# A hybrid backbone block: the context's split input moves to GLA's workspace, and its projections are computed together with those of segments 0 and 1

## The chip, the cores and the metric

The kernel runs on one core of one Trainium2 chip. Its time is the device time in microseconds. PE is TensorE, DVE is VectorE, ACT is ScalarE, POOL is GpSimd, SP is SyncE, whose queue issues most of the DMAs.

## The reference, cut to what matters

One layer works on 2048 latent tokens and on a context of 256 tokens, 1024 features each. Both are normalized, modulated by an adaLN vector (context and latent have their own) and multiplied by one combined input matrix. Its columns feed three mixers: gated linear attention (GLA: q, k, v, decay ranks, gate gg), a gated linear recurrence with a short convolution (RG-LRU: lx, gate lg) and a state-space layer (S5: su).

```python
for d in range(N_DIR):
    ...
    yc, h_ctx = run(d, ci, None)      # the context is scanned alone
    yl, _ = run(d, li, h_ctx)         # the latent scan starts from its final state
```

After the mixers come an output projection, a second norm and an MLP with squared ReLU. The context's own outputs are not needed, so of its columns only su, lx, v and k are computed.

## The kernel before, in words

The tokens are cut into the context "c" (256 tokens) and segments 0 to 3 of 512 tokens. Features lie on partitions, in eight tiles of 128 (KT). Every operand of a large product is split into two fp32r parts, high and low, and a product of 1024 features by 128 columns is 8 x 3 = 24 matmuls (`mm3`, L323 to L326: high x high, high x low, low x high).

**The input's preparation** (`h_of`, `hprep`): 256 tokens are loaded (L287), squared on ACT (L291), summed on DVE (L292, L294), summed over partitions on PE (L296), made into a factor on ACT (L298, L299); DVE multiplies (L302), ACT writes the high part hH (L303), DVE the low part hL (L307). A segment takes two such halves, the context one. The load tile x has one buffer, so a half is loaded only when the half before it is finished. hH and hL come from `big_pair()`, two buffers each, and the context takes one of the two.

**The weights** (`wsplit`): a tile of 128 x 1024 (512 KB) is loaded by SP (L318), its high part written by ACT (L319), its low part by DVE (L320). There are two buffers for the load and the high part, three for the low part.

**The order of the work.** `in_proj` is the main stream: it goes through a plan, a list of (names, chunks) written by hand; ("h", s) prepares a chunk, and every other entry computes for each name, and in it for each chunk, one weight tile's product into one of two PSUM tiles acc. v0 and v1 are computed token block by token block (272 columns: 256 values and 16 decay ranks). Side streams (S5's preparation `s5_prep`, GLA's `gla_prep`, RG-LRU, `mod_rest` with the rest of the adaLN weights) are woven in by the time that the main stream has yielded, and each waits for the names of the chunks that it reads. The scheduler of the language then fixes one order for each engine; priorities (HP, WP) put preparation and weight splits ahead. What comes later (read-out, output projection, MLP) follows the first phase.

**GLA's workspace.** `wg` hands out tiles of 128 x 1024 floats, four buffers (YS). `gla_prep` takes three of them for the context and four for each pair of blocks; for a pair it runs L895 on PE, then ACT, DVE and POOL, then transposes L928 on PE. `gla_prep("c")` is the first of GLA's stream and needs v0, v1, k0 and k1 of the context.

Of the kernel before, what the change touches and what calls it, by code (L numbers as in the profile page):

```python
# [8 lines left out]
F32 = mybir.dt.float32  # L9
# [7 lines left out]
P = 128  # L17
D = 1024
KT = 8
# [4 lines left out]
NS = 16          # S5 groups  # L24
T8 = 8           # tokens that share a column of the S5 input layout
T16 = 16         # S5 chunk
NCH = SEQ // T16  # latent chunks
CCH = CTX // T16  # context chunks
NP = T16 + 2     # powers of the transition
XSZ = 1312  # L30
PKW = 1408       # S5 matrices of a group: read-out 2 x 256, input 4 x 128, kernel 3 x 128
# [11 lines left out]
# columns of the packed per-feature vector table  # L43
# [9 lines left out]
# W_in column tiles of 128 features  # L53
COLS = ["su0", "su1", "lx0", "lx1", "k0", "k1", "q0", "q1", "gg0", "gg1", "gg2", "gg3", "lg0", "lg1"]
WIDX = {n: i for i, n in enumerate(COLS)}
VN = 272         # half of v and the decay ranks of one direction


class Streams:
    """Emits a main and several side streams of instructions in step.  # L60

    A stream yields the time that its step takes, or the name of an event that has to be emitted first."""
# [10 lines left out]
    def step(self, limit):  # L73
        """One step of the side stream that is furthest behind; False if none is ready before `limit`."""
        ready = [x for x in self.live if (x[3] is None or x[3] in self.done) and (limit is None or x[2] <= limit)]
        if not ready:
            return False
        x = min(ready, key=lambda y: y[2])
        x[3] = None
        try:  # L80
            r = next(x[0])
        except StopIteration:
            self.live.remove(x)
            return True
        if isinstance(r, str):
            x[3] = r
        else:
            x[2] += r * x[1]
        return True

    def run(self, main):
        """`main` with the side streams."""
# [20 lines left out]
def chain(*gens):  # L113
    for g in gens:
        yield from g
# [3 lines left out]
def hybrid_block(ctx: ExitStack, tc: tile.TileContext, xT, ctxT, cc, cct, wmodA, wmodT, pv, win, wva, wvb, upw, lrini, lruw, s5v, gluw,  # L119
# [27 lines left out]
    # ---------------------------------------------------------------- constants  # L147
# [14 lines left out]
    gsc1 = consts.tile([P, 16], F32, name="gsc1")      # norm1*(1+sc1): latent, context  # L162
    gsc2 = consts.tile([P, 8], F32, name="gsc2")

    # DRAM scratch, one tile per token segment
# [22 lines left out]
    qq_d = dram.tile([8, P, 1024], F32, name="qq_d")      # by pairs of blocks  # L188
    kk_d = dram.tile([8, P, 1024], F32, name="kk_d")
    ds_d = dram.tile([NB, 64, 512], F32, name="ds_d")      # backward block updates  # L190
    sf_d = dram.tile([16, 64, 512], F32, name="sf_d")      # forward states that enter the blocks
    bs_d = dram.tile([64, 512], F32, name="bs_d")          # backward state carried to the next segment
    # constant rows and borders of the scratch
# [7 lines left out]
    # ---------------------------------------------------------------- pools of the first phase  # L201
# [4 lines left out]
    def slots(tag, size, bufs):  # L206
        """A rotating workspace of `bufs` slots of `size` floats a partition."""
# [19 lines left out]
    def big_pair():  # L227
        """The two parts of a split operand of 512 tokens."""
# [4 lines left out]
    # ---------------------------------------------------------------- adaLN vectors  # L233
# [3 lines left out]
    # silu(c) on every partition, for the products that run along the free axis  # L237
# [8 lines left out]
    def mod_first():  # L246
        """shift and scale of the first norm, latent and context"""
# [35 lines left out]
    # ---------------------------------------------------------------- normalized, modulated, split input  # L283
    def hprep(pool, src, t0, n, hH, hL, gsc, sh):
        """Normalize and modulate n tokens of src and split them exactly into two fp32r parts."""
        x = pool.tile([P, KT, n], F32, name="x", tag="x", bufs=XB)
        S.dma_start(x, src[:, t0:t0 + n].rearrange("(k p) t -> p k t", p=P))  # L287
        # 1/rms over the features on every partition
# [20 lines left out]
    def wsplit(pool, src, shape, tag, bufs, parts=None):  # L309
        """Load a weight tile and split it exactly into two fp32r parts (in `parts`, if they are there already);  # L310
        bufs: of the load, of each part."""
# [16 lines left out]
    # ---------------------------------------------------------------- input projection  # L328
# [30 lines left out]
    def h_of(s):  # L359
        n = seg_n(s)  # L360
        hH, hL = (t[:, :, :n] for t in big_pair())
        hh[s] = (hH, hL)
# [6 lines left out]
    def v_cols(c, chunks):  # L369
        """Half of the values, token by token, with the decay ranks of one direction."""  # L370
# [50 lines left out]
    # ---------------------------------------------------------------- RG-LRU  # L421
# [21 lines left out]
    def lru(d, order, wl=wl):  # L443
        for s in order:
# [31 lines left out]
            # gates; sigmoid(z) = (1 + tanh(z/2))/2  # L476
# [35 lines left out]
    # ---------------------------------------------------------------- S5  # L512
# [4 lines left out]
    def s5_params():  # L517
# [73 lines left out]
        def cmul(or_, oi, ar, ai, br, bi, t, conj_b=False, neg_i=False):  # L591
            """(or, oi) = a*b (conj(b) if conj_b); oi negated if neg_i."""
# [51 lines left out]
        # step[k] = e^{+-i theta T 2^k}: + on the forward half, - on the backward half  # L644
# [7 lines left out]
        # input matrix  # L652
# [20 lines left out]
        # powers by slot: E: forward j, backward 17-j;  F: forward 15-s, backward s  # L673
# [13 lines left out]
    def s5_prep(b):  # L687
# [5 lines left out]
        # C lambda^k by slot  # L693
# [22 lines left out]
        # intra-chunk kernel, both directions  # L716
# [11 lines left out]
        # shifted windows of it make the Toeplitz blocks  # L728
# [9 lines left out]
    def s5_tables(g0):  # L738
        """Phase tables of four groups by doubling."""
# [23 lines left out]
    def s5_run(g):  # L763
# [32 lines left out]
        # real scans; results shifted by one chunk so that a chunk's column holds the state that enters it  # L796
# [9 lines left out]
        # the state that enters latent chunk c sits at column c + CCH + 1 on both halves  # L806
# [25 lines left out]
    # ---------------------------------------------------------------- GLA, first part: decays and block states  # L832
# [18 lines left out]
    def gla_prep(s, blocks, other=False):  # L851
        """Decays, decayed queries and keys, block updates, forward states of pairs of blocks of a segment.

        other: in the memory that the input's norm has left."""
# [15 lines left out]
        for b in blocks:  # L870
# [19 lines left out]
            # -log_sigmoid(z) = max(-z, 0) + log(1 + exp(-|z|))  # L890
# [49 lines left out]
            # forward states  # L940
# [16 lines left out]
    def gla_ends():  # L957
        """-log_sigmoid of the (shifted) token past the end of each sequence"""
# [15 lines left out]
    # ================================================================ read-out and MLP  # L974
# [15 lines left out]
    def ws(s, n, tag="t"):  # L990
        """Workspaces of the read-out, n tiles of 512; the last segment's come before the MLP's memory is there."""
# [11 lines left out]
    def decays():  # L1003
        # exponents of the decay between a block's anchor and the state that enters it
        # forward: -c_mid/16; backward: -(c_127 - c_mid + c_0 of the next block)/16
# [14 lines left out]
    def back_step(ss, blk):  # L1020
        """backward state that enters latent block blk -> ss[64:128]"""
# [17 lines left out]
    def open_ff():  # L1039
        """The first phase's workspaces make room for the MLP's."""  # L1040
# [8 lines left out]
    def read_out(s):  # L1049
        """Read-out of the three groups of a segment."""  # L1050
# [6 lines left out]
        # GLA read-out, pairs of blocks from the last to the first as the backward state runs  # L1057
# [55 lines left out]
        # RG-LRU gate  # L1113
# [14 lines left out]
        # S5 gate  # L1128
# [24 lines left out]
    def out_proj(s):  # L1153
        """Output projection, residual and second norm of a segment."""
        early = []
        if s == 3:
            # the first products run while the S5 group's read-out comes to its end
# [33 lines left out]
        # second norm; its split result takes the place of the split read-out  # L1191
# [102 lines left out]
    # ================================================================ first phase  # L1294
# [149 lines left out]
```

## Time and profile before

| | |
|---|---|
| median of 3 runs | 2480.51 us (2476.4 to 2482.62) |
| profiled execution, its span | 2482.1 us, nothing around it |
| PE busy | 2347.2 us, 95%, 10992 matmul records |
| PE weight loads busy | 1886.0 us, 76% |
| DVE busy | 1610.0 us, 65% |
| ACT busy | 1169.2 us, 47% |
| POOL busy | 100.7 us, 4% |
| PE share of the chain that ended last | 64% |

The profiled execution lies 1.6 us above the median and within the runs. Busy shares are means over a first phase (to about 850 us), in which all engines work, and the MLP after it, which is nearly all PE.

### The profile page before, as it was taken

The numbers are of one execution on the slowest core, as the hardware profiler recorded it, in microseconds if no ns is written. First come the engines' busy times: TensorE is split into PE (matmuls) and PEld (weight loads), VectorE is DVE, ScalarE is ACT, GpSimd is POOL, SyncE is SP. The second block draws the span as 40 slices with busy tenths as digits, with TensorE's granted clock in tenths as the row PEclk, the third lists the DMA queues.
The fourth block names the chain that finished last, engine by engine and source line by source line (L and its number), as shares of the span: only waits on it lengthen the run. The fifth ranks groups of instructions, "written<-read, shape, count | busy, mean of one in ns | idle before, by whom it ended". The sixth has DMA issues, their size and how long they took to land.

```text
span 2482.1 us, 29891 instructions
## 1 busy us (share of the span) xinstructions
PE 2347.2 (95%) x10992; PEld 1886.0 (76%) x10992; DVE 1610.0 (65%) x2698; ACT 1169.2 (47%) x1704; POOL 100.7 (4%) x141
## 2 busy tenths in 40 slices
PE   7779999898887899999999999999999999999997
PEld 3668777877675677888877788887778888888886
DVE  6886878726786766565576656557655655655555
ACT  3764567436555645343355534336543433433333
POOL 1020111002100000000000000000000000000000
PEclk9989999999998999999999999999999999999999
DMA  7666777557775643322355322336522232333221
GB/s 258 209 201 208 223 238 227 168 174 207 253 240 181 206 135 120 101 94 93 100 177 162 118 86 93 102 102 202 159 85 94 94 102 87 126 102 102 94 94 51
DMA packets 189107, 364.03 MB, mean 147 GB/s; under 512 B 35200, under 2 KB 104144, under 8 KB 187920
## 3 DMA queue, kind: packets, MB, share of 16 engines
q1 hardware_dynamic: 183872, 346.20, 44.1%
q0 software_dynamic: 5088, 15.93, 1.9%
q8 instruction: 86, 1.41, 0.2%
q14 instruction: 61, 0.50, 0.1%
HBM read 299.76 MB, written 62.75 MB: 146 GB/s over the span
## 4 chain that ended last, share of the span: by engine, by line
PE 64%; ACT 5%; DVE 5%; DMA 3%; issue 2%; SPq 1%; POOL 0%; DVEq 0%; ACTq 0%; POOLq 0%
PE acc L324 10%; PE acc L326 9%; PE acc L325 9%; PE sa L324 9%; PE sa L325 9%; PE sa L326 9%; PE sb L324 2%; PE sb L326 2%; PE sb L325 2%; DVE wL L320 1%; ACT wH L319 1%; PE sb L1146 1%; DMA t<-lru 1%; DMA t<-kk_d 0%; DMA wR<-in_wout_dram 0%
## 5 line engine op out<-in xcount | busy, mean ns | idle before, releaser
L319 ACT CAST wH<-wR 128x1024 fp32r<-128x1024 f32 (+1 forms) x353 | 370.9, 1051 | 903.9 <-PE sa L325 432.8
L324 PE MATMUL acc<-hH,wH 128*128 128x512 f32 (+1 forms) x1576 | 629.6, 400 | 24.8 <-ACT hH L303 9.2
L320 DVE TENSOR_TENSOR wL<-wR,wH 128x1024 fp32r<-128x1024 f32 (+1 forms) x353 | 427.3, 1222 | 346.5 <-ACT wH L319 342.0
L326 PE MATMUL acc<-hH,wL 128*128 128x512 f32 (+1 forms) x1576 | 620.1, 394 | 3.2 <-DVE wL L320 3.1
L325 PE MATMUL acc<-hL,wH 128*128 128x512 f32 (+1 forms) x1576 | 617.7, 392 | 1.2 <-DVE hL L307 0.8
L1257 DVE SCALAR_TENSOR_TENSOR xa<-sa,modl,xa 128x512 f32<-128x512 f32 (+1 forms) x520 | 383.1, 741 | 197.5 <-PE sa L326 194.8
L324 PE MATMUL sa<-sH,wH 128*128 128x512 f32 (+1 forms) x1040 | 403.9, 389 | 4.6 <-DVE xa L1257 4.2
L326 PE MATMUL sa<-sH,wL 128*128 128x512 f32 (+1 forms) x1040 | 402.2, 387 | 0.0
L325 PE MATMUL sa<-sL,wH 128*128 128x512 f32 (+1 forms) x1040 | 401.9, 386 | 0.0
L324 PEld LDWEIGHTS acc<-hH,wH 128*128 128x128 f32 x1576 | 299.8, 191 | 95.3 <-ACT hH L303 10.3
L325 PEld LDWEIGHTS acc<-hL,wH 128*128 128x128 f32 x1576 | 300.1, 191 | 70.8 <-issue 6.2
L326 PEld LDWEIGHTS acc<-hH,wL 128*128 128x128 f32 x1576 | 299.5, 190 | 70.8 <-DVE wL L320 5.2
L324 PEld LDWEIGHTS sa<-sH,wH 128*128 128x128 f32 x1040 | 195.2, 188 | 49.2 <-DVE xa L1257 9.3
L326 PEld LDWEIGHTS sa<-sH,wL 128*128 128x128 f32 x1040 | 195.3, 188 | 40.8
L325 PEld LDWEIGHTS sa<-sL,wH 128*128 128x128 f32 x1040 | 195.4, 188 | 40.6 <-DVE sL L1233 0.8
L1233 DVE TENSOR_TENSOR sL<-sr,sH 128x512 fp32r<-128x512 f32 x128 | 88.2, 690 | 27.6 <-ACT sH L1232 27.5
L325 PE MATMUL acc<-wL,hH 128*128 128x272 f32 x288 | 87.8, 305 | 8.8 <-DVE wL L320 8.7
L324 PE MATMUL acc<-wH,hH 128*128 128x272 f32 x288 | 89.2, 310 | 2.0 <-ACT ev L331 1.9
L331 ACT COPY ev<-acc 128x512 f32<-128x512 f32 (+2 forms) x96 | 47.5, 495 | 85.1 <-issue 41.0
L326 PE MATMUL acc<-wH,hL 128*128 128x272 f32 x288 | 86.5, 301 | 0.0
L1232 ACT CAST sH<-sr 128x512 fp32r<-128x512 f32 x128 | 78.8, 617 | 10.8 <-PE sa L326 9.0
L1231 ACT ACTIVATE sr<-sr 128x512 f32<-128x512 f32 x128 | 80.8, 632 | 3.4
(402 smaller groups left out, 2717.2 us busy)
## 6 DMA issues: line engine op xcount, KB each, us to landing
wR<-in_w_dram SPq DMA_DIRECT2D x256, 512.0 KB
wR<-in_win_dram SPq DMA_DIRECT2D x54, 512.0 KB
wm<-in_wmodT_dram SPq DMA_DIRECT2D x32, 512.0 KB
wR<-in_wout_dram SPq DMA_DIRECT2D x32, 512.0 KB
wm<-in_wmodA_dram SPq DMA_DIRECT2D x8, 1024.0 KB
x<-in_xT_dram SPq DMA_DIRECT2D x8, 1024.0 KB
w<-pk_d SPq DMA_DIRECT2D x16, 512.0 KB
xa<-in_xT_dram SPq DMA_DIRECT2D x32, 256.0 KB
```

Source lines behind the costliest of these rows:

```text
L319: A.copy(Hf, raw)
L320: V.tensor_tensor(Lf, raw, f32(Hf), OP.subtract)
L324: T.matmul(acc, wH, hH, start=first, stop=False)
L325: T.matmul(acc, wH, hL, start=False, stop=False)
L326: T.matmul(acc, wL, hH, start=False, stop=last)
L331: A.copy(e, acc)
L1146: T.matmul(ps, gw[:, k, ct * P:(ct + 1) * P], sg[k], start=k == 0, stop=k == 1)
L1231: A.activation(r, r, AF.Square)
L1232: A.copy(sH, r)
L1233: V.tensor_tensor(sL, r, f32(sH), OP.subtract)
L1257: V.scalar_tensor_tensor(xa[:, m, a0:a1], acc, modl[:, 40 + m:41 + m], xa[:, m, a0:a1], OP.mult, OP.add)
```

## The change: what it does

The context's hH and hL no longer come from `big_pair()`. They are put into GLA's four wg tiles, each part in two halves of four feature tiles, which the new class `Halves` indexes like one tile. Segments 0 and 1 so have both big pairs from the start. The plan is rewritten: A4 (su0 su1 lx0 lx1) runs for the context and segment 0 with one split of each weight tile, v0 v1 k0 k1 for the context, segment 0 and segment 1, then q0 q1 for segments 0 and 1, and then A4 for segment 1. From G4 of segment 0 on the plan is as before. Other lines of the diff only drop comments.

```diff
+class Halves:
+    def __init__(self, tiles):
+        self.tiles = tiles
+    def __getitem__(self, at):
+        p, k, t = at
+        if isinstance(k, slice):
+            return Halves([x[p, :, t] for x in self.tiles])
+        return self.tiles[k // 4][p, k % 4, t]
...
     def h_of(s):
         n = seg_n(s)
-        hH, hL = (t[:, :, :n] for t in big_pair())
-        hh[s] = (hH, hL)
+        if s == "c":
+            hh[s] = [Halves([side.tile([P, KT // 2, CTX], F32R, name="wg", tag="wg", bufs=YS) for _ in range(2)]) for _ in range(2)]
+        else:
+            hh[s] = big_pair()
+        hH, hL = hh[s]
...
-    st.run(chain(in_proj([("h", "c"), ("h", 0), (A4 + " v0 v1 k0 k1", ["c"]), ("h", 1), (A4, [0]), (A4, [1]),
-                          (B6, [0, 1]), (G4, [0]), ("h", 3), (G4, [1]), ("h", 2), (A4, [3]), (B6, [3, 2]), (A4, [2]),
+    st.run(chain(in_proj([("h", "c"), ("h", 0), (A4, ["c", 0]), ("h", 1), ("v0 v1 k0 k1", ["c", 0, 1]), ("q0 q1", [0, 1]), (A4, [1]), (G4, [0]), ("h", 3), (G4, [1]), ("h", 2), (A4, [3]), (B6, [3, 2]), (A4, [2]),
                           (G4, [3]), (G4, [2])]),
```

How the instructions stand: both programs have 10,248 instructions on PE, and the last 8,104 of them stand in the same order. So do the last 1,743 of DVE, 1,239 of ACT and 645 of SP. At the end of B6 of segments 3 and 2 (and already at the point where the set su, lx, v, k, q of the context, 0 and 1 is complete) both orders hold the same number of instructions of every kind on PE. DVE has 10 instructions fewer, and SP 10 DMAs fewer.

PE before, behind the first products of su0 for the context (acc_640): su1 for the context follows at once, in acc_674, woven into it.

```order
L324 MATMUL acc_640<-hH_507,wH_635 128x256
L325 MATMUL acc_674<-hL_508,wH_669 128x256
L326 MATMUL acc_674<-hH_507,wL_670 128x256
L324 MATMUL acc_674<-hH_507,wH_669 128x256
L325 MATMUL acc_640<-hL_508,wH_635 128x256
```

PE now, at the same place: acc_642 is su0 for the context (wg_507 to wg_510 are its input's parts), acc_670 su0 for segment 0 (hH_560), acc_708 su1 for the context. Lines 337 to 339 are `mm3`, 309 the norm's sum, 729 to 740 `s5_prep`.

```order
L338 MATMUL acc_642<-wg_510,wH_637 128x256
L339 MATMUL acc_642<-wg_508,wL_638 128x256
L309 MATMUL mm_571<-ssum_564,ones_65 128x256
L729 MATMUL sa_744<-ident_70,w_736 128x128 x4
L729 MATMUL sa_751<-ident_70,w_736 128x128 x4
L739 MATMUL sa_852<-w_548,w_168 16x256
L740 MATMUL sa_852<-w_548,w_168 16x256
...
L309 MATMUL mm_608<-ssum_601,ones_65 128x256
...
L337 MATMUL acc_670<-hH_560,wH_637 128x512
L337 MATMUL acc_708<-wg_507,wH_703 128x256
```

Between the context's first tile and all its others there now stand the norm's two sums of segment 0, one whole `s5_prep` and the first product of 512 columns, which reads both halves of segment 0.

DVE before, around the norm's sums of segment 0's second half (L292, L294): two weight splits (L320) stand among them.

```order
L292 TENSOR_TENSOR ssum<-ssum,sq 128x1024
L602 TENSOR_TENSOR w<-w 128x576
L294 TENSOR_TENSOR ssum<-ssum 128x512
L320 TENSOR_TENSOR wL<-wR,wH 128x1088
L294 TENSOR_TENSOR ssum<-ssum 128x256
L320 TENSOR_TENSOR wL<-wR,wH 128x1024
```

DVE now, at the same place (L305, L307 are the sums, L291 is `mod_rest`, L619 to L624 `s5_prep`):

```order
L619 TENSOR_TENSOR w<-w 128x2x256
L620 TENSOR_TENSOR w<-w 128x2x256
L305 TENSOR_TENSOR ssum<-ssum,sq 128x1024
L624 TENSOR_TENSOR w<-w 128x512
L307 TENSOR_TENSOR ssum<-ssum 128x512
L291 SCALAR_TENSOR_TENSOR wm,modl<-wm,cbl 128x1024
L307 TENSOR_TENSOR ssum<-ssum 128x256
```

Weight splits no longer stand there; `s5_prep` and `mod_rest`, which came later before, have moved up into their place.

## Rows read from the trace of the kernel before

**Rows 1.** Windows: length, busy PE, PEld, DVE, ACT, POOL (instructions), PE clock, DMA share, GB/s.
```profile
43.80:98.40 54.60, 36.82 (x227) 33.69 (x227) 49.16 (x145) 41.08 (x67) 2.92 (x4) 0.84 0.56 184
98.40:153.00 54.60, 44.27 (x196) 33.01 (x196) 48.62 (x88) 39.05 (x64) 8.58 (x10) 0.91 0.69 224
153.00:290.40 137.40, 133.06 (x776) 111.03 (x777) 103.11 (x223) 65.28 (x110) 15.54 (x19) 0.99 0.68 205
290.40:545.20 254.80, 235.30 (x1216) 191.69 (x1215) 169.99 (x324) 139.18 (x219) 36.52 (x48) 0.95 0.68 208
```

**Rows 2.** Chain of waits on PE, 43.8 to 153 us: total, times, longest.
```profile
PE acc L324 <- ACT hH L303: 9.2, 2, 5.6
PE acc L325 <- DVE wL L320: 7.8, 3, 5.4
PE mm L296 <- DVE ssum L294: 3.7, 1, 3.7
PE acc L324 <- ACT ev L331: 3.7, 3, 1.7
```

**Rows 3.** Windows as in rows 1, four stretches in which products take twice as long.
```profile
47.50:54.40 6.90, 6.08 (x27) 5.78 (x28) 6.90 (x33) 5.39 (x9) 0.00 (x0) 0.51 0.02 7
68.20:71.40 3.20, 3.20 (x14) 3.20 (x15) 1.06 (x4) 2.61 (x5) 0.00 (x0) 0.50 0.79 230
78.30:81.70 3.40, 3.40 (x15) 3.40 (x16) 3.40 (x10) 0.59 (x2) 0.00 (x0) 0.51 0.99 320
143.30:146.50 3.20, 3.18 (x7) 2.26 (x8) 3.20 (x9) 2.36 (x6) 0.00 (x0) 0.50 0.85 295
```

**Rows 4.** Timeline of SP's queue and VectorE, 54 to 149 us: start, length.
```profile
54.68 0.38 SPq L287 DMA_DIRECT2D x<-in_xT_dram  x1
...
70.59 1.67 DVE L302 SCALAR_TENSOR_TENSOR x<-x,gsc,ssum 128x256 f32<-128x256 f32 x4 [2.14 <-ACT ssum L299]
...
75.34 1.66 DVE L307 SCALAR_TENSOR_TENSOR hL<-x,modl,hH 128x256 fp32r<-128x256 f32 x4
...
77.04 0.38 SPq L287 DMA_DIRECT2D x<-in_xT_dram  x1
...
99.31 0.39 SPq L287 DMA_DIRECT2D x<-in_xT_dram  x1
...
124.14 0.38 SPq L287 DMA_DIRECT2D x<-in_xT_dram  x1
...
148.69 0.38 SPq L287 DMA_DIRECT2D x<-in_xT_dram  x1
```

**Rows 5.** Timeline of PE: products of 256, 272, 16 x 256 and 512 columns.
```profile
63.91 0.28 PE L325 MATMUL acc<-hL,wH 128*128 128x256 f32 x1
64.03 0.28 PE L326 MATMUL acc<-hH,wL 128*128 128x256 f32 x1
...
83.03 0.29 PE L324 MATMUL acc<-wH,hH 128*128 128x272 f32 x1
83.16 0.29 PE L325 MATMUL acc<-wL,hH 128*128 128x272 f32 x1
...
113.33 0.62 PE L722 MATMUL sa<-w 64*16 64x256 f32 x4
...
258.72 0.39 PE L326 MATMUL acc<-hH,wL 128*128 128x512 f32 x1
258.95 0.39 PE L324 MATMUL acc<-hH,wH 128*128 128x512 f32 x1
```

**Rows 6.** Groups by line and form, 43.8 to 481 us: weight splits, busy, mean ns.
```profile
L320 DVE TENSOR_TENSOR wL<-wR,wH 128x1024 fp32r<-128x1024 f32 x32 | 38.9, 1216 | 19.1 <-ACT wH L319 19.1
...
L319 ACT CAST wH<-wR 128x1024 fp32r<-128x1024 f32 x32 | 33.5, 1048 | 18.7 <-PE acc L325 15.8 <-DMA wR<-in_win_dram 1.7 <-PE acc L326 1.2
```

**Rows 7.** Timeline of PE around GLA's first block of segment 0.
```profile
282.92 1.99 PE L895 MATMUL sb<-glt,upt 48*128 48x256 f32 x8
...
308.28 1.94 PE L928 MATMUL sb<-ident,wg 128*128 128x128 f32 x8 [4.99 <-issue]
```

## The prediction

> **What bounds the kernel now.** I read the windows first, since the change touches only the beginning. From 43.8 us, where the first norm begins, to 98.4 PE is busy 36.82 of 54.60 us and to 153.0 44.27 of 54.60; then it is nearly full to 290.4 and 92% busy to 545.2 [rows 1]. PE is the engine that everything waits for in the end, so what I count is PE's lost time: idle time, and half of the busy time in which its clock is at the lower of its two levels (0.5 of 2.4 GHz). The last 8,104 PE instructions stand in the same order before and now, and up to there both orders hold the same work; so the difference of the two times is the difference of lost time in this first part, and what comes behind it is shifted as a whole.
>
> The chain of waits says what PE lacked up to 153 us: the input's high part for 9.2 us in two waits (3.6 for the context at the start, 5.6 for segment 1 late), the low part of a weight tile 7.8, the norm's sum 3.7, an evacuation 3.7 [rows 2]. In four stretches the clock was at 0.5 and PE was busy 6.08, 3.20, 3.40 and 3.18 of them [rows 3]: together 15.9 us, so 7.9 lost. With 17.8 and 10.3 us of idle time, before loses 36.0 us from 43.8 to 153. Behind that it loses 4.3 + about 1.4 to 290.4, and 19.5 + about 11 (the clock's 5%, less the idle time in it) to 545.2 [rows 1].
>
> The timeline of the preparation is the other thing to see. The four loads of x that follow the first stand 22.4, 22.3, 24.8 and 24.6 us apart [rows 4], since the tile has one buffer: each half of a segment is loaded, summed, scaled and split before the next is loaded. Segment 0 was there at about 99 us, segment 1 at 148.7. Before fills the first wait with the context's other seven tiles; that is why PE is two thirds busy there.
>
> **The change part by part.** *Removed:* ten weight splits (su0 su1 lx0 lx1 once more, v0 and v1 with two tiles each, k0 k1). At 1.22 us on DVE and 1.05 us on ACT [rows 6] that is 12.2 and 10.5 us, and ten loads of about 0.5 MB. DVE is 90% busy up to 153 (97.8 of 109.2 us [rows 1]), so this counts only in so far as PE waited for it: the 7.8 us for low parts go, and the cycles of the preparation may shrink. *Also gone:* segment 1 is wanted much later than it is ready, so its 5.6 + 3.7 us go with the half clock behind them.
>
> *Moved:* the context's seven tiles. In the new order PE has one of them (su0) and then stands before su0 of segment 0, which reads 512 columns, so both halves. PE takes its instructions in order, so nothing behind can fill the time; between stand only one S5 preparation and two sums. What the seven tiles are worth: 24 products at 0.12 us for 256 columns are 2.9 us, at 0.125 for a block of 272 3.0 [rows 5]; three tiles, four blocks and two tiles are 26.5 us. Before did nearly all of it by 98.4; now it comes behind.
>
> How long PE stands: up to the load of segment 0's first half at 54.7 us nothing is different. Two cycles follow. I take 23.4 us for one: the 22.3 seen, and 1.1 for what the new order puts into it (a `mod_rest` pass of DVE among the sums, whose weights are loaded behind x on the same queue; S5's products ahead of the second sum on PE). The second half is then finished at 101.5. The first product may begin with its first high part, some 5.4 us earlier (about 1 us behind 70.59, against 77.0 [rows 4]): 96.1. Bounds: a cycle without one split on each engine, 22.3 - 2.3 = 20.0, gives 89.3; one as slow as 24.7 gives 98.7.
>
> The context's su0 ends at about 54.3, with 3.6 us of waiting and 3.0 of half clock as before. From there to 96.1 are 41.8 us, less S5's 24 records at 0.155 [rows 5] and the sums, about 4.2: 37.6 lost. Behind a wait of this kind the clock was at 0.5 for 3.2 to 6.9 us [rows 3]: 2.5 lost. Until the first block of v PE then waits perhaps 1.4 us for the norm's sum behind a weight split, and 1.0 for the second weight tile of v, whose buffer comes free only when lx1 is done. Sum: 3.6 + 3.0 + 37.6 + 2.5 + 2.4 = 49.1, and 0.8 for the first low part as before makes **49.9 us lost where before lost 36.0: +13.9**.
>
> *Costed at nothing:* segment 1's two halves end near 125 and 149, and the first block of v that needs them comes at about 152 (96 + 31 for the rest of A4, three tiles of 2.9 and four of 24 x 0.23 [rows 5], 18 for the six blocks ahead, some 7 of side work); if they were 10 us later PE would wait that much. GLA's context preparation begins some 90 us later, because k1 of the context does and because wg is taken until then; nothing reads GLA's states before the read-out of segment 3, and the order has as much GLA work in by the end of the first set as before. RG-LRU of segment 1 waits for A4 of segment 1, again ahead of its use. `Halves` doubles no instruction: the parts are written and read one feature tile at a time.
>
> *Later waits:* I take the 36 us that before loses from 153 to 545.2 as the same now. The largest kind is GLA's transposes: L928 began 25.4 us after L895, with 4.99 us of idle PE before it [rows 7]. In the new order some 20 us of products stand between the two for the context, 18 and 22 in two later pairs, and over 29 in the others; before had, counted by the same prices, about 20, 28, 28, and one of 16 that did not wait. So some pairs wait more, some less: -8 to +8.
>
> The Trainium skill (Perfetto Trace Analysis, Identifying the Most-Contended Engine and Optimization Strategy) says to take the engine of the highest occupancy in a regime and to relieve it first. In this regime that is DVE at 90%, and the change does relieve it; by the rule the time falls. Against it stands what PE waits for here: a load with one buffer and a chain over four engines, in which DVE's own share of a cycle can be cut by one split.
>
> All together 2482.1 + 13.9 = 2496.0 in the profiled execution, which stands 1.6 above the median of the runs; against the median, **2494**.
>
> **The rivals.** *Not slower, because the cycles shrink.* Without the splits both cycles take 20.0 us, PE begins at 89.3, and the two small waits do not occur: 13.9 - 6.8 - 2.4 = +4.7, 2485. For it: splits stand inside every cycle before. Against it: other work has moved into their place in DVE's order.
>
> *Faster, because DVE's relief reaches the later waits.* The S5 preparation and `mod_rest` run in the hole, so DVE and ACT are some 8 to 10 us ahead from there, and the chains behind GLA and the weight tiles end earlier. It decides the sign once more than half of the later 36 us go as well as the 6.8: with 24 gone, 13.9 - 6.8 - 24 = -17, 2464. For it: 7.8 us of waits for low parts and GLA's 4.99 end on DVE. Against it: from 153 on DVE is busy 75% and 67% [rows 1]; those waits are of an order fixed in advance. The Trainium skill's rule above (Identifying the Most-Contended Engine) is for this case.
>
> *Slower still, by GLA.* If its chain takes 25 us each time, the three short distances cost 5, 7 and 3 us and a half clock behind each, some 8 more than before: +22, 2503.
>
> *No change at all*, because the seven tiles still run in the hole, would need PE to take them ahead of su0 of segment 0; the order excludes it.
>
> **How the numbers follow.** About 0.3%, 7 us, is what a measurement can tell from no change. I give the forecast (own range 2486 to 2503) 0.53, the early start 0.22, the faster case 0.13, GLA's 0.12. The early start lies within 0.3%, as does a small part of the forecast: faster 0.13, same 0.25, slower 0.62. The range leaves out about one in ten on either side: 2473 to 2507.
>
> **What would show it.** After: one gap of some 40 us on PE from about 54 us, broken only by S5's and the norm's products and ended by ACT's high part of segment 0; no waits for low parts up to 150, none for segment 1; DVE less busy there, ten splits fewer; the first S5 run (and all behind) about 14 us later, with the same waits. The prediction is wrong if the gap ends before 88 us, if segment 1 or v's evacuations are waited for, or if the lost time from 153 to the end of B6 differs from 36 us by over 10.

## The result

| | before | after |
|---|---|---|
| median | 2478.45 us (4 runs, 2476.18 to 2482.62) | 2492.09 us (4 runs, 2488.6 to 2494.11) |
| profiled execution | 2482.1 us | 2492.3 us |
| PE busy | 2347.2 us, 95% | 2341.3 us, 94% |
| DVE busy | 1610.0 us | 1600.8 us |
| ACT busy | 1169.2 us | 1160.7 us |

The change makes the kernel slower: ratio 1.0056, interval 1.0042 to 1.0069, 13.9 us of 2480. The whole shift is there before the common tail of the order begins: the 1968th of the large products ends at 545.2 us before and at 558.9 after, and the next wait that both share, in front of S5's first run, is 5.41 us long in both, 13.6 us later in the second. That product, before and after:

```profile
544.85 0.39 PE L326 MATMUL acc<-hH,wL 128*128 128x512 f32 x1
```

```profile
558.47 0.39 PE L339 MATMUL acc<-hH,wL 128*128 128x512 f32 x1
```

The two profiled executions end 10.2 us apart and not 13.6: behind this product the second takes 3.4 us less. Over all kernels of this document that tail lies between 1929 and 1938 us, so the difference says nothing.

The windows of after, in the columns of [rows 1]. The third ends where the first set of products is complete (the 1008th product, at 303.5; before at 290.6).

```profile
43.80:98.40 54.60, 19.93 (x70) 12.98 (x71) 47.15 (x144) 30.66 (x51) 0.92 (x1) 0.56 0.40 132
98.40:153.00 54.60, 51.82 (x330) 46.91 (x329) 40.83 (x82) 33.77 (x62) 4.86 (x7) 1.00 0.70 217
153.00:303.50 150.50, 142.14 (x804) 119.00 (x803) 106.98 (x223) 75.41 (x121) 16.91 (x27) 0.97 0.59 181
```

Against [rows 1] PE loses 17 us of busy time up to 98.4 and wins 7.6 back up to 153. The chain of waits on PE from 43.8 to 153 us in after:

```profile
PE sa L729 <- DVE w L613: 14.8, 1, 14.8
PE mm L309 <- DVE ssum L307: 12.5, 2, 10.8
PE acc L337 <- ACT wg L316: 3.6, 1, 3.6
PE sa L729 <- DVE w L624: 2.8, 1, 2.8
PE acc L337 <- ACT hH L316: 1.9, 1, 1.9
PE acc L337 <- ACT ev L344: 1.1, 2, 0.9
```

Of [rows 2] are left the context's 3.6 us, 1.7 of the norm's sum and 1.1 for evacuations (ACT's copies of finished PSUM tiles): no wait for a weight's low part, none for segment 1's high part. In their place stands one wait in pieces. The timeline of PE, from the end of su0 for the context on:

```profile
55.06 0.41 PE L339 MATMUL acc<-wg,wL 128*128 128x256 f32 x1
66.28 1.22 PE L309 MATMUL mm<-ssum,ones 128*128 128x256 f32 x2 [10.80 <-DVE ssum L307]
82.32 1.11 PE L729 MATMUL sa<-ident,w 128*128 128x128 f32 x4 [14.82 <-DVE w L613]
86.23 1.11 PE L729 MATMUL sa<-ident,w 128*128 128x128 f32 x4 [2.80 <-DVE w L624]
...
89.11 1.22 PE L309 MATMUL mm<-ssum,ones 128*128 128x256 f32 x2
...
93.68 0.50 PE L337 MATMUL acc<-hH,wH 128*128 128x512 f32 x1 [1.92 <-ACT hH L316]
94.02 0.28 PE L337 MATMUL acc<-wg,wH 128*128 128x256 f32 x1
```

From 55.5 to 93.7 us PE has only the norm's two sums and one S5 preparation, and the first product of 512 columns ends the gap; what it waited for at last is ACT's high part. The name in a row is not the cause of the gap: at 82.32 S5's transposes waited for DVE, but all large products behind them in the order need segment 0's second half or stand behind one that does. The one at 94.02, su1 for the context, is of the second kind. DVE had made the last low part of its weights and of its input long before:

```profile
40.29 1.23 DVE L333 TENSOR_TENSOR wL<-wR,wH 128x1024 fp32r<-128x1024 f32 x1 [3.27 <-ACT wH L332]
...
53.76 0.48 DVE L320 SCALAR_TENSOR_TENSOR wg<-x,modc,wg 128x256 fp32r<-128x256 f32 x1
```

So its operands were there by 54.3 us, a PSUM tile was free at 55.9 (ACT's copy of su0), and it ran 38 us later, right behind the product that the order has ahead of it. The loads of x in after, on SP's queue:

```profile
54.27 0.38 SPq L300 DMA_DIRECT2D x<-in_xT_dram  x1
...
76.23 0.38 SPq L300 DMA_DIRECT2D x<-in_xT_dram  x1
...
99.05 0.37 SPq L300 DMA_DIRECT2D x<-in_xT_dram  x1
...
122.97 0.40 SPq L300 DMA_DIRECT2D x<-in_xT_dram  x1
...
146.75 0.38 SPq L300 DMA_DIRECT2D x<-in_xT_dram  x1
```

They stand 22.0, 22.8, 23.9 and 23.8 us apart, beside 22.4, 22.3, 24.8 and 24.6 [rows 4]: the two cycles of segment 0 are no shorter without the splits among them. PE's chain of waits in after, from 153 to 303.5 us:

```profile
PE acc L338 <- DVE wL L333: 2.7, 1, 2.7
PE sb L945 <- issue: 2.6, 1, 2.6
PE mm L407 <- ACT ev L344: 1.8, 1, 1.8
PE acc L337 <- ACT wH L332: 1.3, 1, 1.3
```

Before waited 2.0, 1.1 and 0.8 us in the same part of the work (153 to 290.4). Three stretches at half clock (3.4 us each, at 173.2, 210.7 and 255.1) lie in this part of after, one in that of before.

### The profile page after: what moved, and what is told of

It is laid out like the page before. It is cut to its first block, busy times and chain, and to the rows that moved or that the text cites. A ratio compares the mean times of both kernels' runs of the same rounds, so it can differ in the third digit from the quotient of the medians.

```text
span 2492.3 us, 29855 instructions
## 1 busy us (share of the span) xinstructions
PE 2341.3 (94%) x10992; PEld 1881.7 (75%) x10992; DVE 1600.8 (64%) x2688; ACT 1160.7 (47%) x1695; POOL 93.9 (4%) x141
## 4 chain that ended last, share of the span: by engine, by line
PE 70%; DVE 7%; ACT 5%; DMA 3%; issue 2%; SPq 1%; DVEq 0%; ACTq 0%
PE acc L337 11%; PE acc L339 11%; PE acc L338 11%; PE sa L337 9%; PE sa L338 9%; PE sa L339 9%; PE sb L337 2%; PE sb L339 2%; PE sb L338 2%; DVE wL L333 1%; ACT wH L332 1%; PE sb L1163 1%; PE sa L800 1%; PE mm L1108 1%; PE sb L912 0%
## 5 line engine op out<-in xcount | busy, mean ns | idle before, releaser
L332 ACT CAST wH<-wR 128x1024 fp32r<-128x1024 f32 (+1 forms) x343 | 360.0, 1050 | 923.5 <-PE sa L338 431.9
L333 DVE TENSOR_TENSOR wL<-wR,wH 128x1024 fp32r<-128x1024 f32 (+1 forms) x343 | 414.9, 1222 | 351.6 <-ACT wH L332 349.0
L337 PE MATMUL acc<-hH,wH 128*128 128x512 f32 x1528 | 615.6, 403 | 14.8 <-ACT hH L1218 6.3
L339 PE MATMUL acc<-hH,wL 128*128 128x512 f32 x1528 | 607.2, 397 | 2.7 <-DVE wL L333 2.7
L338 PE MATMUL acc<-hL,wH 128*128 128x512 f32 x1528 | 601.6, 394 | 0.5 <-DVE hL L1033 0.4
L337 PEld LDWEIGHTS acc<-hH,wH 128*128 128x128 f32 x1528 | 289.1, 189 | 85.4 <-issue 8.1
L338 PEld LDWEIGHTS acc<-hL,wH 128*128 128x128 f32 x1528 | 289.5, 189 | 69.3 <-issue 5.6
L337 PEld LDWEIGHTS sa<-sH,wH 128*128 128x128 f32 x1040 | 195.2, 188 | 46.7 <-DVE xa L1274 6.8
L1249 ACT CAST sH<-sr 128x512 fp32r<-128x512 f32 x128 | 78.9, 617 | 10.8 <-PE sa L339 9.0
L337 PE MATMUL acc<-wH,hH 128*128 128x272 f32 x256 | 78.8, 308 | 0.9 <-ACT ev L344 0.9
L1247 ACT ACTIVATE sr<-acc 128x512 f32<-128x512 f32 x128 | 75.3, 589 | 2.9 <-PE acc L339 2.9
L337 PE MATMUL sb<-hH,wH 128*128 128x512 f32 x192 | 75.8, 395 | 0.0
```

The costliest lines, as they stand in the source:

```text
L332: A.copy(Hf, raw)
L333: V.tensor_tensor(Lf, raw, f32(Hf), OP.subtract)
L337: T.matmul(acc, wH, hH, start=first, stop=False)
L338: T.matmul(acc, wH, hL, start=False, stop=False)
L339: T.matmul(acc, wL, hH, start=False, stop=last)
L1247: A.activation(r, acc, AF.Relu)
```

## The experiments

**The theory.** PE takes its instructions in order; after the context's first tile the next thing in its order that can run needs both halves of segment 0, and these come when the chain of the preparation gives them, not when DVE has less to do. The loss is the context's work that no longer stands in that gap. (Of a plan, the edits below show only the part that differs. mm, sa and sb are the PSUM tiles of the side work.) **The rivals:** the workspace (GLA's tiles are held by the context, GLA comes late), and the saved splits (DVE's relief is worth much, whichever sign it has in the sum).

One table for all runs: the ratio to the kernel before and what it is in us of 2480, and PE's idle time in two windows of the same length for all (109.2 and 447 us, less busy PE). The second window holds the rest of the first phase up to about S5's first run; since the work in a window shifts with the time, a difference of 3 or 4 us in a column means nothing.

| kernel | ratio (interval) | us against before | idle 43.8 to 153 | idle 153 to 600 |
|---|---|---|---|---|
| before | 1 | 0 | 28.1 | 29.8 |
| after | 1.0056 (1.0042 to 1.0069) | +13.9 | 37.5 | 39.7 |
| e1_storage | 1.0000 (0.9989 to 1.0011) | 0 | 28.5 | 32.7 |
| e2_a4hole | 1.0023 (1.0013 to 1.0033) | +5.7 | 30.9 | 35.0 |
| e4_split2 | 1.0059 (1.0046 to 1.0071) | +14.6 | 35.6 | 35.8 |
| e3_vkhole | 1.0058 (1.0045 to 1.0070) | +14.4 | 32.7 | 39.4 |
| e3_pt | 1.0024 (1.0012 to 1.0036) | +6.0 | 22.4 | 38.4 |
| nr_after | 1.0018 (1.0007 to 1.0029) | +4.5 | 34.2 | 32.9 |
| nr_before | 0.9955 (0.9939 to 0.9971) | -11.2 | 21.2 | 27.8 |
| q_after | 1.0169 (1.0147 to 1.0191) | +41.9 | 54.6 | 35.4 |
| q_before | 1.0085 (1.0063 to 1.0106) | +21.1 | 35.9 | 41.4 |
| e6_gg | 0.9958 (0.9945 to 0.9972) | -10.4 | 20.6 | 34.6 |
| gg_pt | 1.0037 (1.0024 to 1.0049) | +9.2 | 20.3 | 46.7 |
| z1_seg0first | 1.0033 (1.0020 to 1.0046) | +8.2 | 32.6 | 43.1 |

### The storage alone

The changed kernel with the plan of before:

```diff
-    ("h", 0), (A4, ["c", 0]), ("h", 1), ("v0 v1 k0 k1", ["c", 0, 1]), ("q0 q1", [0, 1]), (A4, [1]), (G4, [0])
+    ("h", 0), (A4 + " v0 v1 k0 k1", ["c"]), ("h", 1), (A4, [0]), (A4, [1]), (B6, [0, 1]), (G4, [0])
```

> The change's storage (context in the workspace tiles, both big pairs free) with the order of before: the context's seven tiles run alone again, ten weight splits come back. Theory (the loss is TensorE standing with no work while segment 0 is prepared): the hole is filled as before, 2478 us, -4 to +4. Rival A (the workspace: four wg tiles held by the context delay GLA and cost the second half of the first set): slower than before by 5 or more, 2484 and up. Rival B (segment 1 had waited for the context's big pair): faster than before by up to 9, as the 5.6 us wait for segment 1's high part goes.

Measured: 1.0000 (0.9989 to 1.0011). The storage by itself costs nothing and gives nothing that 2.7 us either way would show; nor had segment 1 waited for the context's big pair. With this order the context leaves the workspace as early as GLA's first step could begin anyway, so what its longer stay in after does to GLA is not tested here. PE's busy time in the windows is that of [rows 1] within 0.2 us, that of the other engines within 0.5:

```profile
43.80:98.40 54.60, 36.65 (x228) 33.25 (x228) 49.45 (x147) 41.23 (x67) 2.92 (x4) 0.87 0.56 183
98.40:153.00 54.60, 44.09 (x196) 32.85 (x196) 49.10 (x90) 39.48 (x66) 8.82 (x10) 0.91 0.70 228
```

The 13.9 us need the new plan.

### Three tiles back into the gap

```diff
-    ("h", 0), (A4, ["c", 0]), ("h", 1),
+    ("h", 0), (A4, ["c"]), ("h", 1), (A4, [0]),
```

> The changed kernel, with only su0 su1 lx0 lx1 for the context alone again (four splits come back); v0 v1 k0 k1 stay shared. Theory: three tiles of 2.9 us return into the hole, 2492 - 8.7 = 2483, up to 2 more if the extra splits make PE wait. Rival (the saved splits of VectorE matter more than the hole): no faster than the changed kernel, 2492 or above. Rival A (workspace or GLA late): the excess over before behind 153 us stays as it is in the changed kernel, about 6 us.

Measured: +5.7 us against before, 8.2 less than after. The estimate by the tiles was 8.7; what the four splits more cost is below what this can tell. The 5.7 us that stay lie behind the beginning: counted as lost time (idle, and half of the busy time at half clock), e2_a4hole loses 37.4 us from 43.1 to 153, before 36.7, after 46.9. Behind 153 it idles 5.2 us more than before. That is close to the 6 us by which the expectation marked rival A. v and k are still shared in it, and GLA's context still comes late; which of these costs the rest, no run separates.

### The splits alone

```diff
-    (A4, ["c", 0]), ... ("v0 v1 k0 k1", ["c", 0, 1])
+    ("su0", ["c"]), ("su0", [0]), ("su1", ["c"]), ("su1", [0]), ... ("k1", ["c"]), ("k1", [0, 1])
```

> The changed kernel's order of products, but every weight tile that the context shares is loaded and split once more for the context: the ten splits come back and nothing moves. It prices the saving by itself. Theory: the hole is set by the input's chain; the ten splits cost 0 to 5 us: 2492 to 2497. Rival (VectorE's relief has real worth, and the hole hides it): 8 us or more slower than the changed kernel, 2500 and up.

Measured: 1.0059 beside 1.0056 for after. Ten loads, ten casts on ACT and ten subtractions on DVE more are worth 0.7 us, less than the intervals can tell from nothing. The gap looks nearly the same (its first product of 512 columns comes at 92.2 us, beside 93.7):

```profile
PE sa L729 <- DVE w L613: 14.8, 1, 14.8
PE mm L309 <- DVE ssum L307: 10.2, 1, 10.2
PE acc L337 <- ACT wg L316: 3.6, 1, 3.6
```

So what the change saves is worth next to nothing in its own order. The way there is not quite the same: with the ten splits the 1008th product ends 4.6 us earlier than in after (298.9), and by the 1968th 1.3 us of that are left. DVE is busy for 88% of 43.8 to 98.4 us here and 86% in after, and it does not set the end. The Trainium skill (Perfetto Trace Analysis, Identifying the Most-Contended Engine) would relieve the most occupied engine first; this trace differs: the relief is worth nothing that can be measured.

### The chain of the preparation

One edit leaves the inverse root out of the norm. In place of its two steps on ScalarE, each with a table load, stands one multiplication by a constant on DVE, which shortens each cycle of the preparation, the later segments' too:

```diff
-        A.activation(r, ps, AF.Ln, scale=1.0 / D, bias=epst[:, 0:1])
-        A.activation(r, r, AF.Exp, scale=-0.5)
+        V.tensor_scalar(r, ps, (0.042 if src is ctxT else 1.0) / D, None, OP.mult)
```

> The changed kernel, with one thing left out of the input's norm: the inverse root (two ScalarE instructions with a table load before each, 2.2 to 2.6 us of each cycle of the preparation) is replaced by one VectorE multiplication by a constant. It shortens the chain of the preparation and nothing else. Theory (the chain of the context and of segment 0's two halves sets when TensorE's wait ends): three cycles, each shorter by about 2.3 us: 2492 - 7 = 2485, and the first product of 512 columns comes at about 87 us in place of 93.7. Rival (side work between the steps sets it): at most 1 us less.

> The same left out of the kernel before. Theory: the context's cycle makes all begin 2.3 us earlier; segment 0's two cycles are covered by the context's tiles and give nothing more; segment 1's wait (9.3 us and half clock behind it), which lies five cycles in, goes: 2481 - 2.3 - 10 = 2469. If segment 1's wait does not depend on the chain: 2478.

Measured: 9.4 us less than after, where 7 were expected, and 11.2 us less than before, where 12 were. PE in the first of the two:

```profile
64.75 1.22 PE L309 MATMUL mm<-ssum,ones 128*128 128x256 f32 x2 [11.29 <-DVE ssum L307]
82.58 1.12 PE L728 MATMUL sa<-ident,w 128*128 128x128 f32 x4 [16.61 <-DVE w L612]
84.11 1.22 PE L309 MATMUL mm<-ssum,ones 128*128 128x256 f32 x2 [0.42 <-DVE ssum L307]
...
89.66 0.79 PE L336 MATMUL acc<-hH,wH 128*128 128x512 f32 x1
```

The gap ends 4.0 us earlier, not the 6.7 that was expected: the last wait in it is for S5's w, and its products fill the rest up to the first product of 512 columns, which waits for nothing. The other 5 us of the gain lie behind 153 us (32.9 against 39.7 idle), and no one wait accounts for them. In the kernel before the same edit shortens segment 1's waits:

```profile
PE acc L323 <- ACT hH L302: 3.2, 1, 3.2
PE mm L296 <- DVE ssum L294: 2.6, 1, 2.6
```

5.8 in place of 9.3 us [rows 2] up to 153, not gone as expected; the sum came out right nonetheless.

The other way at the chain was steps of 128 tokens with two load tiles (the sums' tiles, and GLA's use of the load tile, are cut to match):

```diff
-RB, MB, XB, OW, MF, LI, GR = 2, 1, 1, 2, 5000, 3, 4
+RB, MB, XB, OW, MF, LI, GR = 2, 1, 2, 2, 5000, 3, 4
...
-            for t in range(0, n, 256):
-                hprep(ip, src, t0 + t, 256, ...)
+            for t in range(0, n, 128):
+                hprep(ip, src, t0 + t, 128, ...)
```

> The changed kernel, with the input prepared in steps of 128 tokens and two load tiles of that size (the same memory), so that a step's load and sums run beside the step before. Theory (the hole lasts as long as the chain of segment 0's preparation, in which 6 us of each 22 us cycle are the load): segment 0 is there 10 to 16 us earlier, 2492 - 13 = 2479, the sum of waits of TensorE up to 98 us falls from 37 to about 24 us. Rival (the side work that the scheduler puts between on VectorE and ScalarE sets the hole's end): no shorter gap, and twice as many small instructions and table loads on ScalarE: 2492 or above.

> The same preparation in steps of 128 tokens, in the kernel before. Theory: segment 0 and segment 1 come 10 and 20 us earlier, the waits for segment 1's high part and sum (9.3 us) go, VectorE and ScalarE get shorter chains; 2480 - 10 = 2470. If the context's tiles already cover the chain, less: 2476. Rival: more small instructions on a VectorE that is 90% busy, 2484.

Both expectations failed, by 44 and 30 us; the times are those of the rivals (2492 and 2484 or above). The load does come early now, but a step of half the size takes nearly half the time of a whole one, since the next thing with one buffer takes its place. ScalarE in q_after, over one and a half steps of segment 0:

```profile
73.49 0.61 ACT L304 ACTIVATE ssum<-x 128x512 f32<-128x512 f32 x1
74.12 1.28 ACT L311 ACT_TABLE_LOAD   x1
...
78.74 1.28 ACT L312 ACT_TABLE_LOAD   x1
...
83.96 0.61 ACT L304 ACTIVATE ssum<-x 128x512 f32<-128x512 f32 x1
```

The squares that are written into ssum follow 10.5 us apart: `ssum` holds the norm's factor until the last multiplication of the step before has read it. Two steps make 21 us, beside 22 for one of 256 tokens, and each has its two table loads and its own sum in PE's order. The context takes two such steps, so PE starts at 57.3 in place of 47.0 us. The load is thus one link of the chain, and not the link that alone holds it.

### v and k in the gap, and the tile that the norm shares

```diff
-    (A4, ["c", 0]), ("h", 1), ("v0 v1 k0 k1", ["c", 0, 1]), ("q0 q1", [0, 1]),
+    ("v0 v1 k0 k1", ["c"]), (A4, ["c", 0]), ("h", 1), ("v0 v1 k0 k1 q0 q1", [0, 1]),
```

> The changed storage; v0 v1 k0 k1 for the context alone stand in the hole, su0 su1 lx0 lx1 are shared by the context and segment 0 (six splits of v and k come back, four stay saved). Theory: four blocks of 3.0 and two tiles of 2.9 us each for v0 v1 k0 k1 (17.8 us in all, and su0's 2.9 moves behind: net 15 us) return into the hole: 2492 - 15 = 2477, and a few us more for waits for v's weight tiles in the hole, which cost nothing there. Rival (VectorE's saved splits are what counts): between before and the changed kernel or above. GLA for the context can start early again, so rival A expects its 6 us back too: 2471.

Measured: +14.4 us, no better than after; the theory's number failed by 18, and the time is the rival's. Its timeline of PE and, below, the evacuation of v1 on ACT:

```profile
68.29 1.22 PE L309 MATMUL mm<-ssum,ones 128*128 128x256 f32 x2 [4.66 <-DVE ssum L307]
87.97 1.11 PE L729 MATMUL sa<-ident,w 128*128 128x128 f32 x4 [18.46 <-DVE w L613]
89.60 1.19 PE L309 MATMUL mm<-ssum,ones 128*128 128x256 f32 x2 [0.52 <-DVE ssum L307]
91.36 0.38 PE L404 MATMUL mm<-ident,ev 128*16 128x128 f32 x1 [0.57 <-ACT ssum L311]
```

```profile
93.19 0.65 ACT L344 COPY ev<-acc 128x272 f32<-128x272 f32 x2
```

v's four blocks ran up to 63.6 us and then PE stood: k0 and k1 came only at 94.3. There is one PSUM tile mm, and the norm's sums and the transposes of v's ranks (L404) take turns in it; with the norm at higher priority both its sums go first. The ranks keep their ev tiles until then, so v1's two blocks could not be evacuated before 93.19 and held both acc tiles. One edit tests this:

```diff
-            pt = mm_tile()[:16, :nb * P]
+            pt = sb_tile()[:16, :nb * P]
```

> The variant with v0 v1 k0 k1 of the context alone in the hole, and the ranks of v transposed into one of the two sb tiles in place of the one mm tile that the norm's sums use too. Theory: in that variant k0 and k1 could not run in the hole, since v's transposes stood behind the norm's second sum in the queue for the mm tile and v's evacuations behind them; with a tile of their own, k0 k1 and su0 stand in the hole (8.7 us more of it are used) and the wait of 18.5 us for S5's w goes: 2495 - 10 = 2485 or less, down to 2478 if v's later blocks gain too. Rival (something else holds the variant back, DVE or the waits behind 153 us): 2492 and above.

Measured: +6.0 us, 8.4 less than e3_vkhole; 2487.9 by the median, 2.9 more than the range named. The 18.5 us wait is gone, idle time up to 153 falls from 32.7 to 22.4, less than before has. So the tile was the cause in the gap. But against before, 5.7 us less idle time up to 153 stand beside 8.6 more behind it.

### Work for PE while segment 1 is prepared

In the kernel before:

```diff
-    (A4, [0]), (A4, [1]), (B6, [0, 1]), (G4, [0]),
+    (A4, [0]), ("gg0 gg1 gg2 gg3", [0]), (A4, [1]), (B6, [0, 1]), ("lg0 lg1", [0]),
```

> The kernel before, with gg0 to gg3 of segment 0 (22 us of products that need nothing of segment 1) moved ahead of su0 su1 lx0 lx1 of segment 1. Theory (what counts is work for TensorE while an input is prepared): the waits for segment 1's high part and its sum, 9.3 us, and the half clock behind them go: 2480 - 11 = 2469. Rival (the waits come back later, since every chain behind GLA and RG-LRU keeps its place on the other engines): 2480, same as before, or slower by a wait for segment 3's input, whose place in the big pair is no earlier.

Measured: 2470.31 us, 0.9958 (0.9945 to 0.9972): 10.4 us faster than before, the fastest here that leaves nothing out. The waits from 98.4 to 153 us, where before has 11.9 us, 9.3 of them for segment 1 [rows 2]:

```profile
PE acc L326 <- DVE wL L320: 3.5, 2, 2.8
PE sb L895 <- DMA glt<-lrt_c: 1.0, 1, 1.0
PE sa L712 <- DVE w L596: 0.5, 1, 0.5
```

The same theory, used where the kernel before had its own gap, gives the time that it predicts. The waits do not add up to it so neatly: PE idles 7.5 us less than before up to 153, and 4.8 more behind it. The Trainium skill (Perfetto Trace Analysis, Optimization Strategy) says to find the gaps on the engine in question and to make what blocks it start sooner or end faster; the 11.2 us of nr_before agree, and the 10.4 here show that other work put into the gap does as well. Together with the other tile for v's ranks:

> The kernel before, with gg0 to gg3 of segment 0 ahead of segment 1's first tiles (2470 us), and the ranks of v transposed into an sb tile in place of the mm tile of the norm's sums. Theory (v's transposes queue for the norm's tile and hold the evacuations in the hole): the waits of 4.7 us for evacuations up to 98 us go: 2466, -3 to +3. Rival (sb is then short for RG-LRU and GLA, which use it): 2470 or above.

Measured: +9.2 us, 19.6 worse than e6_gg, though up to 153 us both idle the same. Its chain of waits from 300 to 580 us:

```profile
PE sb L928 <- issue: 16.9, 2, 13.1
```

GLA's transposes, for which e6_gg waits 3.8 us in that window, now wait 16.9. The rival named gave the time; the trace does not bear out its reason, that sb is short. PE, DVE and ACT around the longer of the two waits:

```profile
451.13 1.09 PE L928 MATMUL sb<-ident,wg 128*128 128x128 f32 x4 [13.09 <-issue]
```

```profile
449.82 1.21 DVE L914 TENSOR_TENSOR wg<-wg 128x1024 f32<-128x1024 f32 x1
```

```profile
436.50 1.14 ACT L898 ACTIVATE wg<-sb 128x512 f32<-128x512 f32 x2
```

The last reader of sb (L898) ends at 437.6, and nothing touches sb from there to 451.1. What the transposes read is the product of L914, which ends at 451.03, 0.1 us before they start. So PE stands for GLA's own chain, which takes 18.2 us from L895 (432.9) to here. In e6_gg the same pair takes 18.7 us and waits for nothing, for 78 large products stand between the two in PE's order; here 3 do. The edit has changed the order, and the wait came with it. Why the order came out so is not shown.

### Sharing without the gap

```diff
-    ("h", "c"), ("h", 0), (A4, ["c", 0]), ("h", 1), ... (A4, [1]), (G4, [0]),
+    ("h", 0), ("h", "c"), ("gg0 gg1 gg2 gg3", [0]), ("h", 1), (A4, [0, "c"]), ... (A4, [1]), ("lg0 lg1", [0]),
```

> The change's storage and all its shared splits, but segment 0 is prepared ahead of the context, and gg0 to gg3 of segment 0 (22 us of products that need only segment 0) run while the context is prepared; su0 su1 lx0 lx1 of segment 0 and the context follow. Theory (the loss of the change is the wait behind the context's first tile, not the sharing): TensorE begins at about 69.5 in place of 47 us (one cycle more), loses some 29 us up to there with the half clock, and then finds work at every point; the gap from 55 to 94 us is gone. Against the changed kernel's 44 us lost up to 98 this is 15 less, and up to 7 more if the later waits of the changed kernel (13.5 us from 153 us to the end of the first set) fall back to before's 6: 2492 - 15 to - 22 = 2470 to 2477. Rival (the sharing itself, or the workspace, costs in the later stages): 2484 or above, since the later waits grow by what the beginning saves.

Measured: +8.2 us, 5.7 less than after, where 15 to 22 were expected. The time is that of the rival (2484 or above: the later waits grow by what the beginning saves). The first half of the theory shows: PE starts at 71.1 us, and waits nowhere for more than 2.1 us from there to 153. Idle time and half of the busy time at half clock make 30.6 us lost from 43.1 to 98.4, beside 44.2 in after: 13.6 less. Up to 153 it is 37.0 beside 46.9, as much as before loses (36.7): so what makes this kernel 8.2 us slower than before lies behind 153, as in e2_a4hole. The chain of waits from 290 to 560 us names places:

```profile
PE sb L945 <- issue: 9.4, 2, 5.7
PE mm L309 <- DVE ssum L307: 4.6, 1, 4.6
PE acc L337 <- ACT ev L344: 3.8, 1, 3.8
```

## Why the prediction was right, and where only its sum was

The sign, the place and the size came out as forecast, 2492.1 for 2494. By its own steps, with the lost time counted as there (idle, and half of the busy time in the stretches at half clock; before's stretches so counted give 36.7 for the 36.0 up to 153, and 6.0 and 30.7 for the two behind; after begins 0.4 us earlier, so it is counted from 43.1):

- **The gap**: forecast from 54.3 to 96.1, measured 55.5 to 93.7. The cycles took 22.0 and 22.8 us, not 23.4, and the last wait is for ACT's high part as named. Lost up to 153: 46.9 for 49.9. Two errors cancel in part there: 37.9 us are idle where 44.4 were forecast, and the half clock costs 9.0 where 5.5 were, as it held through nearly the whole gap. The step's mechanism holds: e2_a4hole gets 8.2 of 8.7 us back with three tiles, nr_after moves the end of the gap with the chain.
- **Splits at nothing**: shown by e4_split2 (0.7 us). The rival of shrinking cycles falls with it, and so does the faster case: neither the gap nor the later waits got shorter by DVE's relief.
- **Storage and GLA's late start at nothing**: e1_storage shows the storage alone. GLA's late start was not tried by itself; e2_a4hole and z1_seg0first, which have it, are slower behind 153.
- **Segment 1 and the small waits**: no wait for its high part; its norm's sum is waited for 1.7 us, at 137.3 (1.4 forecast). v's evacuations, priced at nothing and named as a sign of being wrong, are waited for after all: 0.9 us at 134.1 and 1.8 at 155.4. The 1.0 us for v's second weight tile did not come there; at 172.6, where v0 gives way to v1, 2.7 us came.
- **Later waits, the same as before**: this step was mis-sized. From 153 to the end of the first set after loses 13.5 us, before 6.0: +7.5, the upper end of the bound of 8, by waits for weight tiles (4.0 us in two), for an evacuation (1.8) and the half clock behind them, besides GLA's (2.6 to 2.0). The 0.6 us more from there to the end of B6 are as forecast only in sum: PE idles 25.4 us for 19.5, and the half clock costs 5.9 for 11.3. GLA's transposes wait 13.4 us up to 558.9 (in five waits) for 9.8 (in three), inside the bound of 8, so the rival of GLA was there in part.

So the sum is 10.2 + 7.5 + 0.6 = 18.3 of lost time, not 13.9, and the time shows 14.0 from PE's first norm sum (0.4 us earlier in after) to the 1968th product. So the step that the same work takes the same busy time failed as well, by 4.3: S5's 128 records of 64 x 256, counted at full clock and without what overlaps, take 20.7 us of PE in before up to there and 16.3 in after, where 117 of them follow another one directly, before 110. The forecast thus hit 13.9 with a beginning 3.7 us too dear (3.0 in after, 0.7 in the count of before), later waits 8.1 too short and a price 4.3 too high. The place and the sign follow from the mechanism; that the three errors cancel to 0.1 us is luck. Why the weight tiles are waited for behind 153 is argued only: with three chunks to a tile, both tiles of v0 are in use until its last block. In e4_split2, with the same order, the same stretch loses 9.7, so it is not fixed to the plan.

What stays open is how the first phase gives back what its beginning wins. Against before, e3_pt idles 5.7 us less up to 153 and 8.6 more behind it, e6_gg 7.5 less and 4.8 more; gg_pt idles as little as e6_gg up to 153 and 12.1 more behind it. nr_after gives nothing back. For one kind of wait the traces name the chain. In before, after, e6_gg, gg_pt and z1_seg0first every wait of over 1 us of GLA's transposes up to 600 us ends 0.06 to 0.11 us behind the same DVE instruction of GLA's chain (L914 in before), also where the row says "issue". How long PE stands there depends on how long that chain takes and on how much other work the order holds between L895 and L928. What decides the waits for weight tiles and for evacuations, no run tells.

## What to carry to other kernels

Sharing a loaded operand between chunks ties the earlier chunk's work to the later chunk's arrival: on an engine that takes its work in order, the work that is moved behind the wait is the price, and it can be counted in tiles before anything is built. Ask first what the saved instructions are worth where they stand; here ten instructions more on an engine that was 86% busy had no measurable effect. Where an input arrives by a chain with one buffer, look for products that need nothing of it and put those ahead: that was worth 10 us here, with no instruction saved. And count on later waits: a better beginning gave part of its gain back in several kernels here, so the waits behind it belong in the sum. Where a row names no releaser, compare the end times of everything that the waiting instruction reads and writes.

## What the runs showed of the hardware and was not expected

- Each cycle of the preparation has two table loads of 1.28 us on ScalarE, whatever its size. A step of 128 tokens takes 10.5 us where one of 256 takes 22, though its load already runs beside the step before: so 256 tokens gained 1 us, and the table loads and the norm's sums in PE's order doubled.
- From 46.9 to 91.2 us of after PE was granted half clock (0.50 in the row, 1.2 of 2.4 GHz) without a break, in 44.3 us of which it was busy for 14.6; it was idle for 3.65 us ahead of that and for 10.8 and 14.8 within. One wait of 1.3 us, at 208.7, was also followed by a stretch at half clock.
- One PSUM tile that two uses share can hold back a third: the norm's sums and v's ranks kept the evacuations waiting in e3_vkhole. With another tile for the ranks a wait of 18.5 us went, and the time fell by 8.4.
